# Two-pass attentions without pass-one sums: values and a ones column moving, outputs by query, in a two-block transformer on one Trainium2 core

## The chip, the cores and the metric

The kernel runs on one core of one Trainium2 chip, in one launch. The metric is device time in microseconds (us), median of the runs. The engines are TensorE (PE, matmuls; its weight loads are PEld), VectorE (DVE), ScalarE (ACT), GpSimd (POOL) and SyncE (SP, which issues most DMAs).

## What is computed

Two blocks over 512 tokens of width 1024, all in f32. The first block has an even layer (attention with 8 heads over 512 tokens and 256 context tokens, beside a convolution) and an odd layer (a recurrence in two directions, beside attention over a neighbourhood), each with adaptive modulation and followed by an expert-choice mixture of 16 experts. The second block has a forgetting attention (16 heads, causal, with a bias from cumulated gates), a feed-forward net, a sparse attention (16 heads, 2 groups of keys; a compressed, a selected and a window branch, each scaled by a gate) and another feed-forward net. Of the attentions this matters:

```
s = q @ k.T * scale            # plus bias, causal mask
p = softmax(s, -1)             # over the keys of one query
o = p @ v                      # by head
o_sparse = g0 * o_c + g1 * o_s + g2 * o_w
mod = silu(c) @ ada_w[i] + ada_b[i]     # six chunks of 1024: sh1, sc1, g1, sh2, sc2, g2
gate, idx = top_k(softmax(h @ router).T, cap)   # routing; g2 * (experts' output) is added to x
```

## The kernel before

One launch runs the stages one after another: the modulation's first chunks and the norm; the inputs of the even layer; the even attention; its output projection; routing and experts (the first mixture); the odd layer; routing and experts; the forgetting attention; a feed-forward net; the sparse attention; a feed-forward net. Matmuls that need f32 accuracy are split into high and low parts in a reduced type (f32r) and made as three products, or are made in f32, which stands in the trace as two matmul records, two passes.

**Two passes of attention.** Scores are needed with queries on the partitions for the maximum and the sum, and with keys on the partitions for the product with V. Pass one (`first`, in `even_first`, `fa_project` and `ns_first`) makes s = -q k by query block i; `Lse.take` (from L506) has DVE make the row's minimum and ACT the exponential of all scores, whose `accum_out` is the row's sum. `Lse.rows` turns -log(sum) - minimum into three bf16 parts, and a matmul with a selector (`add`, L542) adds them to the scores of pass two, so that the exponential of pass two is normalised already. Pass one takes the high and the low product of each score: KA and KL in the later attentions (L766 and L767, L1161 and L1162), three products of high and low parts in the even one (L1471 and, for context queries, L1474). Pass two (`second`) makes scores by key block j (L797 to L799, L1193 to L1195, L1500), the exponential PT on ACT, 128 keys by up to 512 queries, and the products: V's 64 columns are stationary, PT moves, and the two heads of a pair write the two halves of the partitions of one PSUM bank:

```
nc.tensor.matmul(ob[0][HALF[u], qs], lhsT=V[jj][:, h * 64:(h + 1) * 64], rhs=t[:, qs], ...)
```

These are L819, L1214, and L1518 and L1521 in the even layer. The bank then holds the output by feature, as the output projection wants it. In the sparse attention the two branches b and the compressed branch (PcT times vc) add up in one bank; the gates are in the row term (`lG`).

**What sets the order.** `attend` weaves pass one of the groups still to come with pass two of those that are through, step by step, with a manual schedule for PE and ACT. `along` and `interleave` weave two generators of steps with a ratio. A projection's PE work stands in the program order of such steps. PT has eight buffers, PSUM banks are named by use: bk, tb and ob.

**Even inputs.** `even_stage` interleaves `even_inputs` with `ada_steps` (L1643): seven modulation chunks, each of two halves of four loads (aw, 512 KB, on SP's queue) and 16 matmul passes a half (L1663). Chunks 2 and 5 go to HBM through a store on POOL's queue and are read back by rows where they are used (`mod_parts`, L1709).

**Routing** (in `moe`). Squares on ACT, the scaling of x for the gather on DVE (L1781), stored to HBM (L1785) on POOL's queue; transposes of x (L1796), logits (L1803, L1811), softmax, then eight rounds of a top-k search on DVE, index matmuls (L1854) and gathers (L1896) on POOL's queue. The experts' weights (mw, 1 MB) are on SP's queue.

**Odd attention** (`odd_attend`). It is woven with the recurrence. For each pair of heads p and query block i, head by head: scores (L2323 local, L2324 context) on the 64 partitions of the head, bias on DVE, maximum, exponential e with its sum on ACT, the sum's reciprocal on the diagonal of a tile dg (POOL, L2332); matmuls of e with dg transpose and normalise in one (L2342), ACT copies (L2344) and the products with V follow (L2355). `Later` puts off the second and third part by some steps.

## Time and profile before

| | us |
|---|---|
| median of 3 runs | 3947.52 (3941.67 to 3952.7) |
| the profiled execution | 3948.89 |
| its span in the trace | 3947.1 |
| PE busy | 3625.0 (92%) |
| DVE, ACT, POOL busy | 2090.8, 1588.8, 491.6 |
| mean granted PE clock | 0.953 |

The stages in the trace of that execution, in us from the start of the span: even inputs 47 to 273; the heads of the even attention and pass one of its first two groups 273 to 366; the rest of the even attention 366 to 504; its output projection to 570; routing to 617 and experts to 1249; odd layer to 1990, in it the odd attention woven with the recurrence from 1591 to 1780; routing to 2026 and experts to 2501; norm and projection of the forgetting attention to 2687, pass one of its first group from 2637 on; its attention to 2791; feed-forward to 3185; keys and queries of the sparse attention to 3298, pass one of its first group to 3361, its attention to 3546, output projection to 3580; feed-forward to the end.

A row of the timeline has the start, the length, the engine, the line, the operation with out<-in by the names of the program, the stationary operand (partitions*columns) and the moving one, a count of like instructions in a run, and in brackets the idle time before with what ended it. Matmuls are pipelined: the distance from start to start is what one costs, its length is more.

### The profile page before, as it was taken

The numbers are of one execution on the slowest core, as the hardware profiler recorded it, in microseconds if no ns is written. First come the engines' busy times: TensorE is split into PE (matmuls) and PEld (weight loads), VectorE is DVE, ScalarE is ACT, GpSimd is POOL, SyncE is SP. The second block draws the span as 40 slices with busy tenths as digits, with TensorE's granted clock in tenths as the row PEclk, the third lists the DMA queues.
The fourth block names the chain that finished last, engine by engine and source line by source line (L and its number), as shares of the span: only waits on it lengthen the run. The fifth ranks groups of instructions, "written<-read, shape, count | busy, mean of one in ns | idle before, by whom it ended". The sixth has DMA issues, their size and how long they took to land.

```text
span 3947.1 us, 53296 instructions
## 1 busy us (share of the span) xinstructions
PE 3625.0 (92%) x21365; PEld 2471.7 (63%) x21365; DVE 2090.8 (53%) x3363; ACT 1588.8 (40%) x2687; POOL 491.6 (12%) x603
## 2 busy tenths in 40 slices
PE   7998997999998989798779888899999998999999
PEld 4666574656564778575533323476788876667887
DVE  4747437777777554646342212564455556425444
ACT  3356534655554632341211000367433336644232
POOL 1442010000001231323010000310000012000000
PEclk8998998999998999898989999999999999999999
DMA  7440037888884361215579999422222230003232
GB/s 239 136 145 17 17 142 284 352 313 348 309 334 176 134 219 39 89 43 162 202 308 399 416 408 411 163 83 91 86 96 95 77 126 17 1 28 114 89 102 70
DMA packets 264344, 678.69 MB, mean 172 GB/s; under 512 B 16048, under 2 KB 142016, under 8 KB 214816
## 3 DMA queue, kind: packets, MB, share of 16 engines
q1 hardware_dynamic: 256832, 653.48, 45.3%
q0 software_dynamic: 7264, 21.80, 1.7%
q8 instruction: 168, 2.75, 0.3%
q14 instruction: 80, 0.66, 0.0%
HBM read 641.86 MB, written 32.83 MB: 171 GB/s over the span
## 4 chain that ended last, share of the span: by engine, by line
PE 47%; DMA 12%; DVE 4%; ACT 2%; issue 1%; POOL 1%; SPq 0%; POOLq 0%; DVEq 0%; ACTq 0%
PE bk L374 31%; DMA mw<-in_moe_w_dram 9%; DMA aw<-in_ada_w_dram 2%; PE bk L2011 2%; PE ob L1214 1%; PE bk L2342 1%; PE tb L1193 1%; PE bk L1663 1%; PE bk L2380 1%; PE tb L542 1%; DVE wl L351 1%; PE tb L1194 0%; PE ob L374 0%; DMA w<-in_a_w_in_dram 0%; PE rb L2547 0%
## 5 line engine op out<-in xcount | busy, mean ns | idle before, releaser
L351 DVE TENSOR_TENSOR wl<-w,wh 128x1024 fp32r<-128x1024 f32 (+2 forms) x157 | 256.4, 1637 | 276.0 <-ACT wh L350 275.5
L350 ACT CAST wh<-w 128x1024 fp32r<-128x1024 f32 (+2 forms) x157 | 215.5, 1375 | 377.5 <-PE bk L374 325.6
L351 DVE TENSOR_TENSOR wpl<-mw,wph 128x1024 fp32r<-128x1024 f32 x256 | 302.0, 1220 | 31.9 <-ACT wph L350 23.2
L374 PE MATMUL bk<-xTh,wh 128*128 128x512 f32 x704 | 274.3, 391 | 6.2 <-DVE xTl L354 6.2
L350 ACT CAST wph<-mw 128x1024 fp32r<-128x1024 f32 x256 | 258.2, 1047 | 49.2 <-PE bk L1938 31.0
L374 PE MATMUL bk<-xTh,wl 128*128 128x512 f32 x704 | 274.4, 390 | 0.0
L374 PE MATMUL bk<-xTl,wh 128*128 128x512 f32 x704 | 274.3, 390 | 0.0
L2011 PE MATMUL bk<-mw,xgT 128*64 128x512 f32 x1024 | 238.7, 602 | 26.7 <-DMA mw<-in_moe_w_dram 25.8
L2047 PE MATMUL bk<-mw,hidT 128*64 128x512 f32 x1024 | 248.5, 612 | 2.9 <-DMA mw<-in_moe_w_dram 2.2
L2011 PEld LDWEIGHTS bk<-mw,xgT 128*64 128x64 f32 x1024 | 70.0, 137 | 179.0 <-issue 126.3
L1938 PE MATMUL bk<-wph,xgPh 128*96 128x512 f32 x512 | 162.3, 397 | 1.3 <-ACT xgPh L1915 1.3
L1938 PE MATMUL bk<-wph,xgPl 128*96 128x512 f32 x512 | 160.6, 395 | 0.0
L1938 PE MATMUL bk<-wpl,xgPh 128*96 128x512 f32 x512 | 158.5, 394 | 0.0
L2047 PEld LDWEIGHTS bk<-mw,hidT 128*64 128x64 f32 x1024 | 72.2, 139 | 136.4 <-issue 124.1
L374 PEld LDWEIGHTS bk<-xTh,wh 128*128 128x128 f32 x704 | 132.7, 188 | 34.1 <-DVE xTl L354 6.6
L374 PEld LDWEIGHTS bk<-xTl,wh 128*128 128x128 f32 x704 | 132.6, 188 | 27.4
L374 PEld LDWEIGHTS bk<-xTh,wl 128*128 128x128 f32 x704 | 132.5, 188 | 27.5
L1896 POOL DMA_INDIRECT xg<-moe_xn,IDX x32 | 31.8, 994 | 878.1 <-PE tb L1908 849.2
L374 PE MATMUL bk<-wl,gTh 128*128 128x512 f32 x352 | 136.9, 389 | 0.0
L374 PE MATMUL bk<-wh,gTh 128*128 128x512 f32 x352 | 136.9, 389 | 0.0
L374 PE MATMUL bk<-wh,gTl 128*128 128x512 f32 x352 | 136.9, 389 | 0.0
L253 POOL TENSOR_TENSOR hr<-hr,mhalf 128x4 f32<-128x4 f32 (+3 forms) x77 | 91.6, 1196 | 260.8 <-DVE hr L485 255.5
(771 smaller groups left out, 8207.5 us busy)
## 6 DMA issues: line engine op xcount, KB each, us to landing
mw<-in_moe_w_dram SPq DMA_DIRECT2D x384, 1024.0 KB, 11.1
aw<-in_ada_w_dram SPq DMA_DIRECT2D x96, 512.0 KB, 4.6
w<-in_f_w_up_dram SPq DMA_DIRECT2D x40, 1024.0 KB, 5.1
w<-in_f_w_down_dram SPq DMA_DIRECT2D x16, 1024.0 KB, 4.9
w<-in_a_w_in_dram SPq DMA_DIRECT2D x24, 512.0 KB, 3.6
w<-in_od_w_in_dram SPq DMA_DIRECT2D x15, 512.0 KB, 4.6
w<-in_ev_w_in_dram SPq DMA_DIRECT2D x12, 512.0 KB, 4.9
rw_bk<-bk SPq DMA_DIRECT2D x8, 768.0 KB, 4.2
```

Source lines behind the costliest of these rows:

```text
L253: return self.nc.gpsimd.tensor_tensor(t, t, self.mhalf[:p].to_broadcast([p, n]), op=ALU.pow)
L350: nc.scalar.copy(h, src)
L351: nc.vector.tensor_sub(l, src, h.bitcast(F32))
L374: self.nc.tensor.matmul(out, lhsT=L[a], rhs=R[b], start=start and n == 0, stop=stop and n == len(pairs) - 1)
L542: self.k.nc.tensor.matmul(s, lhsT=self.k.selb[0:self.nr, h:h + 1].to_broadcast([self.nr, 128]), rhs=LT, start=False, stop=stop)
L1193: nc.tensor.matmul(s[:, q0:], lhsT=KA[:, b, kv, sl], rhs=QA[:, h, q0:], start=True, stop=False)
L1214: nc.tensor.matmul(o[HALF[u], 128 * jj:], lhsT=V[jj][:, b, kv * 64:(kv + 1) * 64], rhs=t[:, 128 * jj:], start=b == 0 and jj == 0, stop=False)
L1663: nc.tensor.matmul(ps[32 * g:32 * g + 32, :], lhsT=k.silc[:, kk, :], rhs=w[:, kk - k0, :], start=kk < 4, stop=kk >= 4)
L1938: at = nc.tensor.matmul(ps[hf], lhsT=t[a][:, kk, :], rhs=parts[b][:, kk % MOE_WK, hf * 512:hf * 512 + 512], start=kk + n == 0, stop=kk + n ...
L2011: nc.tensor.matmul(ps[64 * hf:64 * hf + 64, :], lhsT=t[:, kk, :], rhs=w[kk // 2][:, kk % 2, hf * 512:hf * 512 + 512], start=kk == 0, stop= ...
L2047: at = nc.tensor.matmul(px[64 * dh:64 * dh + 64, :], lhsT=hTx(q, c), rhs=w2[q][:, c, dh * 512:dh * 512 + 512], start=q + c == 0, stop=q + ...
L2342: nc.tensor.matmul(ps[rr, j * 128:(j + 1) * 128], lhsT=e[:, c0:c0 + n], rhs=dg, start=True, stop=True)
```

## The change

1. `Lse` becomes `Least`. Pass one keeps the high product alone and only takes minima; exponentials, sums and logarithm go. The row term is minus the minimum.
2. V gets a 65th column of ones. `Outs.products` has the 128x128 blocks of PT stationary and the 65 columns of V moving, one matmul for each query block and key block (`o`, 65 columns a query block). The sum stands in the last column. `over` makes the reciprocal on DVE (with the gate in the sparse attention), a DVE product writes a tile O by query, and `turn` transposes O on PE a few steps later and splits it. In the sparse attention each branch has its own pair of banks, the compressed branch comes as products by query in two further banks, and four multiply-adds a head and branch on DVE sum up. PT has 6 buffers (even layer 4), the later attentions have 2 banks bk and 4 ob, and the output projection uses ob.
3. `EV_FIRST`: twelve steps of the even inputs come before the first modulation step. Chunk 5 of layer 0 leaves them and is made in the first routing (`gates`).
4. Routing: transposes and logits stand first in the program, one pow for all squares, the scaling of x is on POOL (128x1024, six and four times).
5. Odd attention: the scores of both heads stand first and alternate between the two halves of the rows; POOL scales e (128x512) by the reciprocal; transposes take the place of the matmuls with the diagonal; values at middle positions are cut so that every block has four whole products.

The diff, cut to its core:

```
-class Lse:
+class Least:
...
-        return lambda: nc.scalar.activation(e, e, AF.Exp, scale=-1.0, bias=mn, accum_out=self.sm[:, h, i:i + 1])
...
-        nc.scalar.activation(t, self.sm[:, h0:h1, :], AF.Ln)
-        nc.vector.tensor_sub(t, t, self.mn[:, h0:h1, :])
...
+        nc.vector.tensor_scalar(t, self.mn[:, h0:h1, :], -1.0, None, op0=ALU.mult)
...
+class Outs:
...
+    def products(self, o, t, v, i0, n, first, last):
+
+        for i in range(n):
+            self.k.nc.tensor.matmul(o[:, 65 * (i0 + i):65 * (i0 + i) + 65], lhsT=t[:, 128 * i:128 * i + 128], rhs=v,
+                                    start=first and i == 0, stop=last and i == n - 1)
+
+    def over(self, o, gate=None):
+
+        nc = self.k.nc
+        v = o[:, 0:65 * self.nt].rearrange("p (i w) -> p i w", w=65)
+        r = self.P.tile([128, self.nt], F32, name="orr", tag="orr", bufs=4)
+        nc.vector.reciprocal(r, v[:, :, 64])
+        if gate is not None:
+            nc.vector.tensor_mul(r, r, gate)
+        return v[:, :, 0:64], r
...
+    def turn(self, bank):
+        nc = self.k.nc
+        for O, dst in self.due:
+            i = 0
+            for h, l, n in dst:
+                ps = bank()
+                for j in range(n):
+                    nc.tensor.transpose(ps[:, j * 128:(j + 1) * 128], O[:, i + j, :], self.k.ident)
+                split_copy(nc, h, l, ps[:, :n * 128])
+                i += n
+        self.due.clear()
...
-                            nc.tensor.matmul(s[:, :n], lhsT=QA[:, h, sl], rhs=KL[:, b, kv, :n], start=False, stop=False)
...
+                    def products(p=p, kv=kv, b=b, j=j, q0=q0, PT=PT, ob=ob):
+                        if j == 0:
+                            ob[:] = [k.obank(), k.obank()]
+                        for u in range(2):
+                            outs.products(ob[u], PT[u][:, q0:], V[j][:, b, kv, :], j, 4 - j, j == 0, j == 3)
                         if b == 0 and j == 0:
...
+                            outs.turn(k.bank)
...
+                                    nc.tensor.matmul(o[:, 64 * i:64 * i + 64], lhsT=PcT[c0:c0 + 32, p // 2, 128 * i:128 * i + 128],
+                                                     rhs=R["vc"][c0:c0 + 32, kv, :], start=True, stop=True)
...
+                    if j < 6:
+                        outs.products(o, t, E.V[j][:, h, :], 0, 4, j == 0, False)
+                    else:
+                        for u in range(2):
+                            outs.products(o, t[:, 256 * u:256 * u + 256], E.V[4 + u][:, h, :], 4, 2, False, u == 1)
...
-                interleave(even_inputs(k, E, hT, cqT, ckT, conv, ws), mods(M), EV_MODS)
+                steps = even_inputs(k, E, hT, cqT, ckT, conv, ws)
+                for _ in range(EV_FIRST):
+                    next(steps)
+                interleave(steps, mods(M), EV_MODS)
...
+            gates = ada_steps(k, Q, layer, (5,), 8, 1024, k.obank) if cs else iter(())
...
+                nc.gpsimd.tensor_scalar(t, x, ss[:, i:i + 1], None, op0=ALU.mult)
+                last = nc.gpsimd.dma_start(xnD[i * 128:(i + 1) * 128, :], t)
...
+            for c0, k0 in ((0, start[i]), (256, 512)):
+                for hd, r in enumerate(HALF):
+                    nc.tensor.matmul(ss[hd][:, c0:c0 + 256], lhsT=O.q[p][r, i * 128:(i + 1) * 128], rhs=O.k[p][r, k0:k0 + 256], start=True, stop=True)
...
+                nc.gpsimd.tensor_scalar(e, e, st[:, 2:3], None, op0=ALU.mult)
...
+                    for j in range(4):
+                        nc.tensor.transpose(ps[:, j * 128:(j + 1) * 128], e[:, j * 128:(j + 1) * 128], k.ident)
...
-        end_x = even_stage(k, lambda P: itertools.chain(ada_steps(k, P, 0, (2, 4, 3, 5), 5), ada_steps(k, P, 1, (1, 0, 2), 5)))
+        end_x = even_stage(k, lambda P: itertools.chain(ada_steps(k, P, 0, (2, 4, 3), 5), ada_steps(k, P, 1, (1, 0, 2), 5)))
```

How the change moves instructions is shown at three places. In these rows a name that ends in a number is a buffer, and a count at the end means so many alike in a run; the line numbers after the change are those of the changed file.

PE in the sparse attention, where the last products of a step stand between pass one (L1161 to L1163) and the next scores of pass two (L1193 to L1195, L542). Before:

```order
L1161 MATMUL bk<-KA,QA 128x128
L1162 MATMUL bk<-KL,QA 128x128
L1163 LDWEIGHTS identb
L1163 MATMUL bk<-causalb,identb 128x128
L1214 MATMUL ob<-PT,V_23540 64x512 x2
L1214 MATMUL ob<-PT,V_23541 64x384 x2
L1193 MATMUL tb<-QA,KA 128x128
L1194 MATMUL tb<-QA,KL 128x128
L1195 LDWEIGHTS causalb
L1195 MATMUL tb<-identb,causalb 128x128
```

PE at such a place with the change; L1200 and L1201 are pass one, L623 the products, L1229 to L1231 and L536 the scores of pass two:

```order
L1200 MATMUL bk<-KA,QA 128x512
L1201 LDWEIGHTS identb
L1201 MATMUL bk<-causalb,identb 128x128
L623 MATMUL ob<-V_23563,PT 128x65 x8
L1229 MATMUL tb<-QA,KA 128x256
L1230 MATMUL tb<-QA,KL 128x256
L1231 LDWEIGHTS causalb
L1231 MATMUL tb<-identb,causalb 128x128
L536 LDWEIGHTS selb
```

The low product of pass one is gone, and the products of two key blocks at a time with 64 stationary columns became, after each key block, one matmul of 65 moving columns for each query block.

PE in the odd attention. L2323 and L2324 are scores, L2342 the products with the diagonal, L2355 those with the values. Before:

```order
L2355 MATMUL bk<-PT,V_11150 64x128 x2
L2355 MATMUL bk<-PT,V_11151 64x128 x2
L2355 MATMUL bk<-PT,V_11152 64x128 x2
L2355 MATMUL bk<-PT,V_11153 64x128 x2
L2342 MATMUL bk<-dg,e 128x128 x8
L2323 MATMUL bk<-kT_11145,qT_11141 128x256
L2324 MATMUL bk<-kT_11145,qT_11141 128x256
L2323 MATMUL bk<-kT_11145,qT_11141 128x256
L2324 MATMUL bk<-kT_11145,qT_11141 128x256
```

PE in the odd attention with the change; L2375 are scores of the two heads in turn, L2393 transposes, L2404 products with the values, L2557 the recurrence:

```order
L2404 MATMUL bk<-PT,Vm_12642 64x128 x2
L2404 MATMUL bk<-PT,Vm_12645 64x128 x2
L2404 MATMUL bk<-PT,V_11155 64x128 x2
L2404 MATMUL bk<-PT,V_11156 64x128 x2
L2557 MATMUL rb<-q_13449,q_13480 32x32 x11
L2393 MATMUL bk<-c_all,e 128x128 x4
L2557 MATMUL rb<-q_13449,q_13480 32x32 x15
L2393 MATMUL bk<-c_all,e 128x128 x4
L2375 MATMUL bk<-kT_11148,qT_11144 128x256 x2
L2557 MATMUL rb<-q_13449,q_13480 32x32 x3
L2375 MATMUL bk<-kT_11148,qT_11144 128x256 x2
```

Eight products with the diagonal became four transposes a head, and the scores of both heads stand together.

POOL's queue in the first routing, up to the gathers (mod_5 is the chunk that the gates g and cg come from, moe_xn the scaled x). Before:

```order
L1785 DMA moe_xn<-xn 128x1024 x6
L1881 COPY Af<-Ax 128x8x64
L1883 COPY Af<-Ac 128x8x32
L1881 COPY Bf<-mod_3_918 128x8x64
L1883 COPY Bf<-mod_3_918 128x8x32
L1709 DMA g_4628<-mod_5 64x512 x2
L1709 DMA cg_4631<-mod_5 32x256 x4
L1896 DMA xg<-moe_xn,IDX 96x1024 x16
```

POOL's queue there with the change:

```order
L1852 TENSOR_SCALAR xn<-c_3856,ss 128x1024
L1853 DMA moe_xn<-xn 128x1024 x6
L1934 COPY Af<-Ax 128x8x64
L1936 COPY Af<-Ac 128x8x32
L1934 COPY Bf<-mod_3_1221 128x8x64
L1936 COPY Bf<-mod_3_1221 128x8x32
L1723 DMA mod_5<-ar 2x512
L1720 DMA ar<-in_ada_b_dram 2x512
L1723 DMA mod_5<-ar 2x512
L1759 DMA g_4631<-mod_5 64x512 x2
L1759 DMA cg_4634<-mod_5 32x256 x4
L1949 DMA xg<-moe_xn,IDX 96x1024 x16
```

The six scalings, the two stores of the chunk and the load of its bias now stand ahead of the gathers on this queue.

## Rows read from the trace of the kernel before

**Rows 1.** Busy us by stretch: length, PE, PEld, DVE, ACT, POOL, clock, DMA, GB/s
```profile
47.00:273.00 226.00, 210.45 (x1071) 136.39 (x1072) 129.98 (x177) 95.05 (x185) 90.37 (x98) 0.92 0.50 160
304.00:366.00 62.00, 52.16 (x292) 43.83 (x291) 51.18 (x108) 45.97 (x95) 22.63 (x33) 0.92 0.08 26
366.00:430.00 64.00, 58.97 (x227) 38.29 (x227) 48.65 (x65) 29.72 (x63) 0.00 (x0) 0.77 0.07 25
570.00:617.00 47.00, 25.44 (x164) 16.73 (x162) 31.87 (x96) 16.58 (x30) 21.33 (x32) 0.69 0.76 290
1591.00:1780.00 189.00, 156.18 (x2388) 129.18 (x2387) 112.02 (x234) 83.53 (x189) 53.14 (x62) 0.89 0.24 69
...
3298.00:3361.00 63.00, 51.14 (x278) 38.91 (x276) 47.99 (x119) 46.13 (x128) 16.26 (x28) 0.92 0.08 26
3361.00:3450.00 89.00, 86.44 (x584) 55.46 (x585) 39.92 (x100) 64.62 (x200) 7.33 (x12) 1.00 0.00 1
```

**Rows 2.** Timeline of PE, 570 to 592: start us, length us, instructions
```profile
571.25 1.96 PE L1770 MATMUL bk<-v,ones 128*128 128x16 f32 x16
...
581.41 0.60 PE L1796 MATMUL ob<-c_all,x 128*128 128x128 f32 x4
```

**Rows 3.** Timeline of PE, sparse attention, 3440 to 3451
```profile
3444.45 0.87 PE L1214 MATMUL ob<-PT,V 128*64 128x256 f32 x8
...
3447.35 0.40 PE L1162 MATMUL bk<-KL,QA 128*128 128x512 f32 x1
3447.59 0.23 PE L1163 MATMUL bk<-causalb,identb 128*128 128x128 bf16 x1
...
3449.19 1.73 PE L1214 MATMUL ob<-PT,V 128*64 128x512 f32 x8
```

**Rows 4.** Waits of PE, 47 to 273: total us, times, longest us
```profile
PE bk L1663 <- DMA aw<-in_ada_w_dram: 7.3, 4, 6.3
```

**Rows 5.** Timeline of PE, modulation chunk 5, 183 to 200
```profile
185.41 3.58 PE L1663 MATMUL bk<-aw,silc 128*32 128x512 f32 x16
...
193.82 0.59 PE L1671 MATMUL bk<-am,c_all 128*2 128x512 f32 x1 [3.23 <-ACT am L1666]
```

**Rows 6.** Even attention by line: duration ns min/median/max, first and last start
```profile
L1471 PE MATMUL wd<-KA,QA x192: 274/392/1415, 304.3 to 428.8; 96*128 96x512 f32 x96, 96*128 96x256 f32 x96
...
L1474 PE MATMUL wd<-KA,QA x48: 274/283/774, 317.6 to 431.8; 96*128 96x256 f32 x48
...
L1518 PE MATMUL bk<-PT,V x96: 592/592/1117, 384.2 to 499.9; 128*64 128x512 f32 x96
...
L1521 PE MATMUL bk<-PT,V x32: 379/379/431, 414.0 to 503.4; 128*64 128x256 f32 x32
```

**Rows 7.** Timeline of POOL, first routing, 570 to 618
```profile
597.43 0.50 POOL L1709 DMA_DIRECT2D cg<-mod  x1 [0.74 <-DMA moe_xn<-xn]
609.34 2.00 POOL L1896 DMA_INDIRECT xg<-moe_xn,IDX  x1 [11.40 <-DVE gtc L1876]
```

**Rows 8.** Waits of PE, first routing, 570 to 617
```profile
PE bk L1854 <- DVE ixf L1850: 11.9, 1, 11.9
```

**Rows 9.** Timeline of PE, odd attention, at 1640 and at 1770
```profile
1639.80 0.70 PE L2323 MATMUL bk<-kT,qT 64*128 64x256 f32 x2
1640.34 0.59 PE L2324 MATMUL bk<-kT,qT 64*128 64x256 f32 x2
...
1770.71 1.16 PE L2342 MATMUL bk<-dg,e 128*128 128x128 f32 x8
```

**Rows 10.** Waits of PE, odd attention, 1591 to 1780
```profile
PE bk L2342 <- POOL dg L2332: 8.6, 5, 3.8
PE bk L2342 <- ACT e L2329: 7.6, 3, 2.9
PE rb L2596 <- DVE x L2587: 6.8, 1, 6.8
```

**Rows 11.** Waits of PE, 3298 to 3361
```profile
PE ob L1161 <- ACT ob L512: 4.5, 4, 1.9
```

More of the change, by code (lines that the diff above doesn't have):

```diff
@@ L567, in simple @@
 def simple(steps):
-    for scores, exps in steps:
+    for scores in steps:
         scores()
-        exps()
         yield
@@ L594, in attend @@
                 now = (i, todo[i][0], todo[i][1])
-                now[2][0]()
+                now[2]()
                 i += 1
@@ L700, in fa_project @@
         nc.gpsimd.tensor_scalar(v[q], k.ident[q, None, 0:1].to_broadcast([64, 8, 512]), 0.0, None, op0=ALU.mult)
-    V = [P.tile([128, D], F32, name=f"V{i}") for i in range(4)]
+    V = [P.tile([128, 16, 65], F32, name=f"V{i}") for i in range(4)]
+    for v in V:
+        nc.gpsimd.memset(v[:, :, 64:65], 1.0)
     ncT = P.tile([128, 4, 16], F32, name="ncT")
@@ L766, in scores @@
                             nc.tensor.matmul(s[:, :n], lhsT=QA[:, h, sl], rhs=KA[:, h, :n], start=True, stop=False)
-                            nc.tensor.matmul(s[:, :n], lhsT=QA[:, h, sl], rhs=KL[:, h, :n], start=False, stop=False)
                             nc.tensor.matmul(s[:, sl], lhsT=k.identb, rhs=k.causalb, start=False, stop=True)
-                            late.append(S.take(s[:, :n], n, h, i, cb[h % 2][:, :n]))
-                    yield scores, lambda late=late: [f() for f in late]
+                            S.take(s[:, :n], n, h, i, cb[h % 2][:, :n])
+                    yield scores
         V_steps = k.dense_steps(xT, range(4), 8, split, [(k.wsrc(W, 2048), 1024, consume(2, 0))])
@@ L921, in shared_kv @@
     R["KL"] = S.tile([128, 2, 2, 512], F32R, name="KL")
-    R["V"] = [S.tile([128, 2, 128], F32, name=f"V{i}") for i in range(4)]
+    R["V"] = [S.tile([128, 2, 2, 65], F32, name=f"V{i}") for i in range(4)]
+    for v in R["V"]:
+        nc.gpsimd.memset(v[:, :, :, 64:65], 1.0)
     R["kcA"] = S.tile([128, 2, 224], F32R, name="kcA")
@@ L957, in consume @@
         pv = ps.rearrange("p (b s c) -> p b s c", b=2, s=2)
-        nc.scalar.copy(R["V"][i], pv[:, :, 1, :])
+        for b in range(2):
+            nc.scalar.copy(R["V"][i][:, b, :, 0:64], pv[:, b, 1, :].rearrange("p (g w) -> p g w", g=2))
         for b in range(2):
@@ L1275, in __init__ @@
         self.cv = P.tile([128, 4, self.CW - 30], F32, name="cv")
-        self.V = [P.tile([128, 512], F32, name=f"V{i}") for i in range(6)]
+        self.V = [P.tile([128, 8, 65], F32, name=f"V{i}") for i in range(6)]
+        for v in self.V:
+            nc.gpsimd.memset(v[:, :, 64:65], 1.0)
         self.KR = P.tile([128, 6, 32], F32, name="KR")
@@ L1804, in moe @@
                     hs = []
+            ss = Q.tile([128, nt], F32, name="ss")
+            xn = [Q.tile([128, D], F32, name="xn", tag="xn", bufs=nt) for _ in range(nt)]
+            for i, (x, t) in enumerate(zip(xs + cs, xn)):
+                nc.scalar.activation(t, x, AF.Square, accum_out=ss[:, i:i + 1])
+            nc.gpsimd.tensor_scalar(ss, ss, 1.0 / D, 1e-6, op0=ALU.mult, op1=ALU.add)
+            last = k.rsqrt(ss)
+            for i, (x, t) in enumerate(zip(xs + cs, xn)):
+                nc.gpsimd.tensor_scalar(t, x, ss[:, i:i + 1], None, op0=ALU.mult)
+                last = nc.gpsimd.dma_start(xnD[i * 128:(i + 1) * 128, :], t)
             lg = k.bank("lg")
@@ L1830, in moe @@
                 nc.scalar.copy(sel[32 * j:32 * j + 16, :], ps[0:16, 0:256])
+            for _ in range(4):
+                next(gates, None)
             val = Q.tile([np_, 64], F32, name="val")
@@ L1876, in moe @@
                 nc.vector.tensor_copy(gtc, ps[:, 0:16])
+            for _ in gates:
+                pass
         Af = P.tile([128, 8, NS], F32, name="Af")
@@ L2819, in fa_stage @@
     load_x(k, X, xD)
-    with k.work("faa", 3, 3, 4, 0, 2, 2, 1024), k.phase("faQ") as Q:
+    with k.work("faa", 3, 3, 2, 0, 2, 4, 1024), k.phase("faQ") as Q:
         fa_attend(k, ops, Q, k.T["a_w_out"], 1)
@@ L2863, in ns_stage @@
             turn = rows(NS_GROUPS[0])
-    with k.work("nsa", 3, 3, 4, 0, 2, 2, 1024), k.phase("nsQ") as Q:
+    with k.work("nsa", 3, 3, 2, 0, 2, 4, 1024), k.phase("nsQ") as Q:
         ns_attend(k, R, lse, first, rows, turn, Q, k.T["b_w_out"], 1, ns_compressed(k, Q, R, 1, k.bank))
```

225 lines of the change are left out of this document (98 added, 127 removed).

## The prediction

> **What bounds the kernel now.** I read the busy time by stretch first, one row per stage. TensorE (PE) is the limit nearly everywhere: 86.44 of 89.00 us in the middle of the last attention, 210.45 of 226.00 in the even inputs [rows 1]. So I ask of each stage whether PE is full; if it is, an instruction taken from PE is worth its own time, and one added costs it. Three stretches are different. In 304 to 366 VectorE (DVE) is busy 51.18 of 62.00 us beside PE's 52.16; in 1591 to 1780 PE has 33 idle us; in 570 to 617 (first routing) it is busy 25.44 of 47.00, and a chain of small steps sets the time [rows 1]. The second routing is the same work for four tiles of x instead of six. Then I read what PE waits for in the stages that the change touches [rows 4, 8, 10, 11], and last the timeline, to price one instruction by the distance between starts.
>
> The prices. An f32 matmul stands in the trace as two passes, and one pass with 128 stationary columns takes 0.112 us however little moves: sixteen passes with 16 moving columns take 1.96 us [rows 2], that is (1.96 - 0.27) / 15, where 0.27 is one pass to its end. By the 0.43 us of 512 moving columns below, 65 need 0.05 and lie inside that, so I take a 65-column product as 2 x 0.112 = **0.224 us**. An f32 transpose is one pass: four in 0.60 us, less the 0.27 of the last, 0.11 each [rows 2]. The form of before keeps the 64 value columns stationary, and two heads run side by side on two column halves: eight passes, four pairs, of 512 columns in 1.73 us, 0.43 a pair, and of 256 in 0.87, 0.22 a pair [rows 3]. The low product of pass one (KL) takes 0.24 us for 512 columns from its start to the next [rows 3]; for fewer columns I scale by columns down to 0.11 (384: 0.18, 256: 0.12, 128: 0.11), 0.65 for the four query blocks of a head.
>
> **The change, stage by stage** (us against the profiled execution's 3948.89).
>
> *Even inputs, -14.* Modulation chunk 5 goes to the routing: 32 passes, of which 16 take 3.58 [rows 5], so -7 on a full PE. A wait for ACT inside it (3.23 [rows 5]) may go too. Twelve input steps now stand before the first modulation step, so PE works while the first weights come: that wait is 6.3 of the 7.3 [rows 4]. I take -7, -6 and -1. Lower end -7 (the wait moves to the next load), upper -20.
>
> *Even heads, 304 to 366, -8.* Pass one drops two of three products: of 192 + 48 passes [rows 6] 128 + 32 go, 64 of 512 columns at 0.24 and 96 of 256 at 0.12, 27 us in all; half of that, 13, lies here. The exponentials of pass one leave ACT. But DVE's minima stay, and 51.18 of 62.00 us [rows 1] is a floor, so at most -11. Bounds -3 and -11.
>
> *Even attention, 366 to 504, +15.* Before: 96 passes of 512 columns in 48 pairs at 0.43 and 32 of 256 in 16 pairs at 0.22 [rows 3, 6]: 24 us. After: 224 products x 0.224 = 50. So +26, and 24 transposes +3, and the other half of pass one -13. Reciprocals and scaling on DVE lie beside PE (DVE 48.65 of 64.00 [rows 1], and that with the convolution, which ends there). 366 to 430 ran at a granted clock of 0.77 [rows 1]; how the new mix is clocked I can't see, so bounds +3 and +28.
>
> *First routing, +5.* The squares' scaling goes from DVE to POOL and logits come first: up to -6, since the top-k chain that PE waits 11.9 for [rows 8] starts sooner. Against it, chunk 5's eight 512 KB loads stand behind eight 1 MB loads on SP's queue, and its two stores and the six gate loads stand on POOL's queue ahead of the gathers. Before, POOL had the gate loads done at 597.43 and sat idle 11.40 us until the first gather at 609.34 [rows 7]. 12.6 MB at the 290 GB/s of this stretch [rows 1] are 43 us, so the weights land at 613 at the latest; part of the first 8 MB comes before 570, and I take 608. Then the last passes, a store, a load and the gather's issue, some 615. Bounds -6 (all inside the idle time) and +12.
>
> *Odd attention, 1591 to 1780, -25.* There are 32 blocks of one head. A block's scores are four f32 passes on 64 rows, 0.54 from the first product to the second, which is alike [rows 9]; now the two heads' products alternate row halves. The trace has no such pair of 256 columns; the nearest are column halves, which do run side by side [rows 3]. So between 0 and half: half, 32 x 0.5 = -17. The normalising matmuls (eight passes, 1.16 [rows 9]) become four transposes at 0.11: about -0.6 each, -19. The diagonal that PE waits for (8.6 [rows 10]) goes; in its place POOL scales 512 columns instead of 128, so that wait may stay. PE had 156.18 busy of 189.00 [rows 1], and its waits on the recurrence (6.8 for x, the largest [rows 10]) get less cover when attention work shrinks. Of 36 I keep two thirds. Bounds -5 and -40.
>
> *Second routing, -3*, the same scaling without a moved chunk. Bounds 0 and -6.
>
> *Forgetting attention, +11.* A head pair's products took 0.87 + 1.73 = 2.6, and take 20 x 0.224 = 4.5 now; they also come in four runs, not two, and a run's end costs some 0.15 (0.60 for four transposes at 0.11 [rows 2]), so 2.2 x 8 pairs = +17.6. Transposes 32 x 0.11 = +3.5; KL 16 heads x 0.65 = -10.4. The projection ahead of it is full of PE work too, so all of KL counts. No output projection is left to fill the last wait: +1 here. Bounds +5 and +16.
>
> *Sparse attention, +16.* Sixteen times 2.2 = +35; transposes +3.5; the compressed branch as eight more products a pair, half of them side by side on row groups, +4 (0 to 8); KL 32 x 0.65 = -21. Before the attention, 3298 to 3361, PE waited on ACT's pass-one exponentials (4.5 for the banks ob alone [rows 11]); these go, DVE is next with 47.99 of 63.00 [rows 1], so -6. Bounds +7 and +24.
>
> The sum is -14 - 8 + 15 + 5 - 25 - 3 + 11 + 16 = **-3**. The profiled execution lies 1.4 above the median of the runs, 3947.52, so I give **3945**.
>
> One rule speaks against the change. The Trainium skill, "TensorEngine Tiling (Array Packing)", section "When to Use Tiling", says that with a moving operand 64 wide or less one should swap, making it stationary, and use two column tiles; that is the form of before. By that rule alone each product doubles, +24 even, 8 x 2.6 = +21 and 16 x 2.6 = +42 instead of the +26, +18 and +35 above, and the sum would be +5, 3953. The rows' prices are what I take.
>
> **Rivals.** A difference of 0.3%, 12 us, is about what a measurement of this kernel can tell from none.
> 1. *Little moves* (3936 to 3959): the attentions' dearer products eat what inputs and odd stage give. For it: the prices of the products are rows of this trace, and gains and losses are of one size. 0.36.
> 2. *PE relief counts in full* (faster). The odd stage follows PE's work to -38, the even inputs reach -20: 13 + 6 more, 3926. For it: in 1591 to 1780 16 us of the waits are the attention's own (8.6 diagonal, 7.6 exponential [rows 10]). Against: these waits have heirs on POOL and ACT. 0.36.
> 3. *The recurrence becomes the bound in 1591 to 1780* (slower). Its chain of DVE and PE steps is woven with the attention; if it needs the 189 us by itself, the removed 36 us turn into waits, and only -5 is left: 3965. It decides once PE's waits for x, q and AMk grow by more than 12 us. For it: 6.8 already waited in one place [rows 10]; against: half of the 33 idle us are the attention's own waits. 0.2.
> 4. *The attentions cost their upper bounds*, because the many short products keep the low clock that 366 to 430 showed: +13, +5 and +8, 3971. 0.08.
>
> That gives faster 0.36, same 0.36, slower 0.28. The bounds all together would reach 3880 to 4012; but they are independent, and adding their half widths by squares (7, 4, 12, 9, 17, 3, 6, 9) gives 27. I leave out a tenth at each end, take 33 for it as some terms can be wrong in kind, and get 3911 to 3977. The likeliest case's own range is 3936 to 3959.
>
> **What would show it.** The distance between two 65-column passes: 0.112 if right, and near 0.06 if weight loads hide, which would take some 70 us (704 products, two passes each) from the sum and make me wrong by far. The stretch of the odd attention about 25 us shorter, waits on POOL's scaling at most 9 us. The sparse attention from its first query pass to the last product 16 us longer. In the first routing a gather at 615 behind the gate loads; if it comes before 609, that term is wrong. PE in the even pass one well under DVE's busy time.

## The result

The changed kernel takes 3994.43 us (median of 4 runs, 3972.86 to 4004.68) against 3949.91 (median of 4 runs of the kernel before): ratio 1.0109, interval 1.0074 to 1.0144, or +43 us. That is 1.1% slower, clear of the noise; I had forecast 3945, 3 us less than before, with a range from 3911 to 3977. The profiled execution of the change took 3999.19 us, 50 more than that of before. From the starts of the first matmuls of each stage in the two traces:

| stage | before | after | difference | predicted |
|---|---|---|---|---|
| even inputs | 224.8 | 215.4 | -9 | -14 |
| even heads and first pass one | 94.2 | 90.1 | -4 | -8 |
| even attention, pass two | 137.5 | 167.4 | +30 | +15 |
| first routing, to the experts' first matmul | 46.0 | 61.5 | +15 | +5 |
| odd stage from the queries on | 554.0 | 551.5 | -2 | -25 |
| second routing | 35.1 | 36.2 | +1 | -3 |
| forgetting attention, pass one to output projection | 179.7 | 179.1 | -1 | +11 |
| sparse attention, pass one to output projection | 275.1 | 293.9 | +19 | +16 |

The rest, some +2, is scattered over stages that the change doesn't touch.

The busy time by stretch of the changed kernel (columns as in [rows 1], counts in brackets): heads and first pass one; pass two in three pieces; first routing; odd attention; sparse attention. In [rows 1] the stretches from 304, 366, 570, 1591 and 3361 answer to them.

```profile
293.00:351.00 58.00, 42.52 (x205) 34.55 (x203) 49.84 (x108) 20.66 (x38) 21.70 (x33) 0.87 0.09 28
...
346.00:421.00 75.00, 69.43 (x240) 53.94 (x241) 49.05 (x67) 11.44 (x18) 0.00 (x0) 0.50 0.02 6
421.00:434.00 13.00, 11.30 (x68) 8.26 (x67) 7.73 (x17) 4.35 (x9) 0.00 (x0) 1.00 0.35 121
434.00:519.00 85.00, 80.77 (x518) 65.23 (x517) 13.94 (x32) 35.00 (x57) 0.00 (x0) 0.96 0.00 1
...
585.00:648.00 63.00, 34.61 (x202) 17.07 (x202) 29.12 (x86) 13.61 (x24) 36.36 (x38) 0.77 0.82 307
1625.00:1802.00 177.00, 145.77 (x2234) 115.85 (x2233) 113.76 (x236) 83.03 (x187) 82.93 (x61) 0.85 0.20 60
3388.00:3480.00 92.00, 88.59 (x712) 73.45 (x721) 47.31 (x165) 30.38 (x72) 7.33 (x12) 0.98 0.01 1
```

Read the clock column of the second row: for 75 us from the start of pass two in the even attention PE had half its clock (0.50, the level of 1.2 GHz), though it was busy 69.43 of them. Before, the stretch from 356 to 387 was at half clock and the next at full:

```profile
356.00:387.00 31.00, 26.30 (x81) 17.90 (x81) 18.51 (x28) 13.35 (x28) 0.00 (x0) 0.50 0.00 1
387.00:421.00 34.00, 29.75 (x150) 18.84 (x148) 31.46 (x44) 20.19 (x42) 0.00 (x0) 1.00 0.00 1
```

The waits of PE in the changed kernel's first routing and odd attention (total us, times, longest us) answer to [rows 8] and [rows 10]:

```profile
PE tb L1961 <- DMA xg<-moe_xn,IDX: 15.5, 1, 15.5
PE bk L1905 <- DVE ixf L1901: 5.5, 1, 5.5
...
PE bk L2393 <- POOL e L2383: 24.4, 14, 4.4
PE rb L2645 <- DVE x L2636: 3.6, 2, 1.8
```

The first routing now waits 15.5 us for the gathered rows, the odd attention 24.4 us for POOL's scaling of e.

### The profile page after: what moved, and what is told of

Read it like the earlier page. It is cut to its first block, busy times and chain, and to the rows that moved or that the text cites. A ratio compares the mean times of both kernels' runs of the same rounds, so it can differ in the third digit from the quotient of the medians.

```text
span 3997.1 us, 54148 instructions
## 1 busy us (share of the span) xinstructions
PE 3660.0 (92%) x21909; PEld 2572.6 (64%) x21933; DVE 2122.8 (53%) x3578; ACT 1432.3 (36%) x2199; POOL 548.8 (14%) x623
## 5 line engine op out<-in xcount | busy, mean ns | idle before, releaser
L2064 PEld LDWEIGHTS bk<-mw,xgT 128*64 128x64 f32 x1024 | 70.1, 138 | 180.7 <-issue 130.5
## 6 DMA issues: line engine op xcount, KB each, us to landing
mw<-in_moe_w_dram SPq DMA_DIRECT2D x384, 1024.0 KB, 10.6
```

Source lines behind the costliest of these rows:

```text
L2064: nc.tensor.matmul(ps[64 * hf:64 * hf + 64, :], lhsT=t[:, kk, :], rhs=w[kk // 2][:, kk % 2, hf * 512:hf * 512 + 512], start=kk == 0, stop= ...
```

## The experiments

Every kernel below is the kernel before with one part of the change, or a part altered, so the differences are against before on the same chip. Below, "low clock" is the time that the profile grants PE 0.50, and 0.1% is 3.9 us.

### The even attention: 2 by 2, and a filler

`even_alone` takes both halves of the change (pass one with minima alone, L1471 to L1474; products of 65 moving columns), `even_one` pass one alone, `even_two` the products alone:

```
 even_one:  Least, scores of the high product alone; products as before
            (the division by the sum is left out)
 even_two:  Lse and three products in pass one as before
-nc.tensor.matmul(ob[0][r, :], lhsT=E.V[jj][:, v], rhs=t, start=jj == 0, stop=jj == 5)
+outs.products(o, t, E.V[j][:, h, :], 0, 4, j == 0, False)
```

> The kernel before with the changed even attention alone (minima in pass one, products of 65 moving columns). In the changed kernel the heads gave -4 us and the attend stage +30. Expected +26 us, within 12, with about 75 us of low clock from the start of pass two on. If the long low clock was an accident of that run, the stage has some 45 us of low clock or less and the total is +12 to +16.

> The kernel before with the even layer's new pass one (minima from the high product) but the products of before, 64 stationary columns in two column halves; the division by the sum is left out. Theory (the short products hold the clock low): the clock recovers some 30 us into the stage as before, -20 to -30 us. Rival (the thinner pass one ahead of it sets the low clock): 70 us or more of low clock here too, -5 to -15 us.

> The kernel before with the even layer's products of 65 moving columns but its old pass one (three products, exponentials and sums stay, the division by the sum comes on top). Theory (the short products hold the clock low once it has fallen): 60 us or more of low clock from the start of pass two, stage of the attend 45 to 55 us longer than before, total +40 to +50. Rival (only the thin new pass one together with them does it): about 30 us of low clock, +26 to +35.

| | ratio (interval) | us | pass two | low clock in it |
|---|---|---|---|---|
| before and fourteen kernels with this stage unchanged | | | 131 to 138 | 20 to 38 |
| even_one | 0.9979 (0.9969 to 0.9989) | -8 | 127 | 30 |
| even_alone | 1.0077 (1.0050 to 1.0104) | +30 | 168 | 76 |
| even_two | 1.0153 (1.0127 to 1.0179) | +60 | 182 | 85 |

The next three fences are the busy time by stretch of pass two, from where the clock fell; read the clock column. First even_alone:

```profile
358.00:432.00 74.00, 69.07 (x240) 53.69 (x241) 48.78 (x67) 10.72 (x17) 0.00 (x0) 0.50 0.01 3
432.00:446.00 14.00, 12.30 (x74) 9.18 (x73) 8.01 (x17) 5.03 (x10) 0.00 (x0) 0.98 0.31 114
```

The same view of even_one:

```profile
352.00:375.00 23.00, 19.25 (x57) 11.28 (x57) 16.56 (x22) 4.95 (x7) 0.00 (x0) 0.50 0.08 24
375.00:486.00 111.00, 102.12 (x429) 53.26 (x427) 48.76 (x79) 44.01 (x74) 0.00 (x0) 0.94 0.04 15
```

And of even_two:

```profile
358.00:450.00 92.00, 86.89 (x306) 70.66 (x307) 50.97 (x73) 32.55 (x67) 0.00 (x0) 0.50 0.01 2
450.00:551.00 101.00, 94.03 (x601) 74.86 (x600) 21.14 (x48) 45.81 (x78) 0.00 (x0) 0.98 0.04 16
```

All three fall to the low clock at the same point, the end of the heads, where PE waits for the last norm on DVE (qn, 2.8 us in even_alone and even_one, 1.1 us in even_two) and a few us later for the row terms. With the old products the clock is back after 23 us; with the 65-column products it stays low for 74 and 92, with the thin pass one and with the old one. So it is the products, not the pass one ahead of them, and the long low stretch is no accident of one run: the changed kernel and even_alone both had 75 us of it, and even_alone's +30 is what I expected. "The products" here means that whole half of the change: with the 65 columns come their order (one key block at a time), the transposes, the division on DVE and 4 PT buffers for 8, and I took none of these apart. I had the sign of even_one right but expected -20 to -30: pass one gave some -6 of its 13 us in pass two and as much ahead of it, and the total (-8, interval -4 to -12) agrees with that. even_two went as its theory had it in clock (85 us low for 60 or more) and stage (50 us over the usual 132); its total, +60, lies above the +40 to +50 expected.

Does the new mix draw the clock down, or does it only fail to bring it back? `even_fill` puts 32 useless matmuls of 512 columns ahead of even_alone's first scores of pass two:

```
+if g == 0 and j == 0 and h == 0:
+    w = k.tbank()
+    for _ in range(32):
+        nc.tensor.matmul(w, lhsT=KA[0:96, 0, 0, 0:128], rhs=QA[0:96, 0, 0, 0:512], start=True, stop=True)
```

> The changed even attention alone, with 32 matmuls of 512 moving columns of no use put before the first scores of pass two (14 us at the low clock). Theory (after dense work the clock is back, and the short products then keep it): the low stretch of 75 us becomes 30 us or less, and the total is 5 to 15 us below that of the same kernel without them, +15 to +25 against before. Rival (the mix itself draws the clock down): low stretch of 60 us or more after the useless matmuls, total +40.

Busy time by stretch of pass two in even_fill:

```profile
363.00:374.00 11.00, 10.86 (x34) 8.69 (x35) 1.36 (x3) 0.00 (x0) 0.00 (x0) 0.70 0.01 1
374.00:417.00 43.00, 35.94 (x225) 27.85 (x223) 41.28 (x57) 9.56 (x16) 0.00 (x0) 1.00 0.00 1
417.00:448.00 31.00, 28.24 (x89) 20.85 (x90) 8.47 (x18) 7.73 (x13) 0.00 (x0) 0.51 0.14 51
```

The clock comes back within the filler and the same mix then runs 43 us at full clock. It falls again at 417, in a wait of PE for the convolution (4.36 us, `L1412 <- DVE cv`), and stays low for 31 us. Pass two without the filler took 152 us instead of 168. The total did not follow: 1.0081 (1.0053 to 1.0110), as even_alone; the filler itself cost 11 us, and its ten runs spread from 3948 to 3999, so I can't say in how many of them the clock did as in this profile. In all four profiles with the new products (the changed kernel, even_alone, even_two, even_fill) the low clock ended 1 to 4 us after a run of f32 matmuls with 512 columns began, those of the convolution's norm; in the changed kernel:

```profile
417.14 5.57 PE L1363 MATMUL tb<-cv,on 128*128 128x512 f32 x8
422.15 0.92 PE L1517 MATMUL wd<-KA,QA 96*128 96x512 f32 x2
```

### The first routing: POOL's queue

`first` has the twelve input steps alone (EV_FIRST), `gates` also moves chunk 5, `route` is the new order of routing with the scaling on POOL alone, `gates_act` is `gates` with the chunk's and the gates' DMAs on ACT's queue:

```
-nc.gpsimd.dma_start(mod[c][:, hf * 512:(hf + 1) * 512], row)
+(nc.scalar if (i, c) == (0, 5) else nc.gpsimd).dma_start(mod[c][:, hf * 512:(hf + 1) * 512], row)
...
-g2 = mod_parts(k, E, mod, 5, 0, 2, "g2")
+g2 = mod_parts(k, E, mod, 5, 0, 2, "g2", nc.scalar if cs else nc.gpsimd)
```

> The kernel before with twelve steps of the even inputs ahead of the first modulation step, chunk 5 still among them. Theory: PE's wait of 6.3 us for the first weights goes and nothing takes its place: -4 to -8 us. Rival: the wait moves to a later load or to the convolution's end: 0, within 3.

> The kernel before with that and with chunk 5 moved into the first routing, the routing's scaling of x still on DVE. Theory (stores and gate loads ahead of the gathers on POOL's queue): even inputs -10, the gather some 15 us later than before, first routing +12 to +16, total +2 to +6 us. Rival (in the changed kernel it was POOL's scaling of x that held the gather): routing within 4 us of before, total -8 us.

> The kernel before with the changed routing alone: scaling of x on POOL, 2.85 us a tile, transposes first, chunk 5 where it was. Theory: six scalings take 17 us, so the stores of x land about 20 us later, after the indices are known, and the gather waits for them: first routing +5 to +12, second routing 0 to +2. Rival (the stores stay inside the top-k's time): -2 to -6 us.

> Chunk 5 in the first routing, twelve input steps first, but the chunk's stores, its bias loads and the gate loads go to ACT's queue instead of POOL's. Theory (these held the gathers up): first routing within 5 us of before instead of +17, total -8 to -12 against before. Rival (PE's second half of the chunk holds the gather's transposes): routing +8 to +12, total within 3 of before.

| | ratio (interval) | even inputs | first routing |
|---|---|---|---|
| before | | 224.8 | 46.0 |
| first | 1.0004 (0.9995 to 1.0014) | 218.8 | 45.1 |
| gates | 1.0022 (1.0006 to 1.0039) | 212.4 | 61.9 |
| route | 1.0004 (0.9986 to 1.0022) | 224.7 | 45.2 |
| gates_act | 0.9990 (0.9970 to 1.0010) | 213.2 | 53.6 |

In `first` the inputs give their 6 us, and the median of its ten runs doesn't show it (+2, interval -2 to +6). Its profile can't say why: it is of the fastest of the ten, 20 us shorter than the profile of before, of which 9 lie in the second experts, which nothing touched. So -4 to -8 for the total is not shown. Moving the chunk gives 6 us in the inputs and costs 17 in the routing, and `gates` is 9 us slower than before (interval +2 to +15). `route` rejects the theory for it that POOL's slow scaling holds the gather; the scaling costs nothing and gains nothing that can be measured. POOL's timeline in the changed kernel shows what does:

```profile
609.18 3.29 POOL L1853 DMA_DIRECT2D moe_xn<-xn  x6
...
625.01 0.55 POOL L1723 DMA_DIRECT2D mod<-ar  x1 [10.69 <-DVE gtc L1927]
628.11 0.51 POOL L1720 DMA_DIRECT2D ar<-in_ada_b_dram  x1 [2.55 <-DMA mod<-ar]
630.95 0.51 POOL L1723 DMA_DIRECT2D mod<-ar  x1 [2.33 <-DVE ar L1722]
631.45 0.85 POOL L1759 DMA_DIRECT2D g<-mod  x1
632.80 0.54 POOL L1759 DMA_DIRECT2D g<-mod  x1 [0.50 <-DMA mod<-ar]
633.33 1.97 POOL L1759 DMA_DIRECT2D cg<-mod  x4
635.61 1.41 POOL L1949 DMA_INDIRECT xg<-moe_xn,IDX  x1 [0.30 <-issue]
```

A store, a bias load that waits until it has landed, a second store, six gate loads, then the gather: 10.6 us of queue, which began some 3 us after the indices were there. The second store waits for a sum on DVE that needs both the bias load (landed at 629.86) and PE's last passes of the chunk (ended at 629.89), so two chains end there together. The gather itself then took 9.7 us from issue to landing, against 5.1 before: some 5 of the 15 us that the routing lost. With these DMAs on ACT's queue (`gates_act`) it lands in 4.4, and it leaves POOL as soon as the indices are there, as the row of POOL's timeline shows. But ACT, which now stands behind the gate loads, casts the experts' weights late, and after them the gathered rows that PE needs:

```profile
590.92 1.01 POOL L2001 DMA_INDIRECT xg<-moe_xn,IDX  x1 [25.86 <-DVE IDX L1971]
```

The row of ACT's timeline, in the same kernel:

```profile
600.15 3.88 ACT L350 CAST wph<-mw 128x1024 fp32r<-128x1024 f32 x4 [6.88 <-DMA g<-mod]
```

So half of the 17 us went, and half became a wait of PE for ACT (7.8 us, `L2043 <- ACT xgPh`). The routing (+8) and the total (-4, interval -12 to +4) came out nearer to the rival than to the theory, but not by the rival's mechanism: PE's passes of the chunk were done (594.3) before the gathered rows were there (595.3).

### The odd attention

`odd_alone` has the changed odd attention alone, `odd_dve` scales e on DVE. `odd_dve_aw` splits the loads of the modulation that is woven behind the attention (ODD_AW) into 256 KB in two buffers, `odd_dve_aw2` has two buffers of 512 KB; the space comes from single buffers in `odd_out`. `aw2` is that alone.

```
-nc.gpsimd.tensor_scalar(e, e, st[:, 2:3], None, op0=ALU.mult)
+nc.vector.tensor_scalar(e, e, st[:, 2:3], None, op0=ALU.mult)
...
-ODD_AW = 1, 1024
+ODD_AW = 2, 1024      # odd_dve_aw: 2, 512
...
-g = mod_row(k, Q, mod, 2, 0, "g", c0, 256, 2)   # and ox 3, ot 2 buffers
+g = mod_row(k, Q, mod, 2, 0, "g", c0, 256, 1)   # and ox 2, ot 1
```

> The kernel before with the changed odd attention alone. Theory: POOL's scaling of e (1.57 us for 128x512 in the changed kernel, 24.4 us of PE waits on it) eats what PE saves: -5 us against before, within 8; PE waits on POOL e about 24 us again. Rival (the recurrence is the bound): also near 0, but the waits stand at the recurrence's x, q and S.

> The same odd attention, e scaled on DVE instead of POOL. Theory: DVE does 128x512 in about 0.4 to 0.5 us, the wait of 24 us goes, -20 to -30 us against before. Rival (recurrence is the bound): within 5 us of the run with POOL, and the waits move to the recurrence's results.

> The changed odd attention with e scaled on DVE, and the modulation weights that are woven behind it loaded in pieces of 256 KB into two buffers instead of 512 KB into one. Theory (what the attention saves is given back as waits for these loads, 25 us): waits on aw fall to 12 us or less, and the total is 8 to 15 us below the run with DVE alone, -18 to -26 against before. Rival (the recurrence's chain is the bound there): waits move to the recurrence, total within 4 us of the run with DVE alone.

> The changed odd attention with e on DVE, the modulation weights in two buffers of 512 KB, so that the two matmuls of a load still run side by side (the pieces of 256 KB made them run one by one, 29 us more of PE). Theory (the attention's gain is given back as waits for these loads): waits on aw under 8 us without more PE time, odd stage 15 to 25 us shorter than with DVE alone. Rival (the recurrence's chain sets the end): odd stage within 6 us of the run with DVE alone.

> The kernel before with these two buffers alone. Theory: waits on aw fall from 22 to under 8 us, -10 to -20 us. Rival: within 4 us of before, the waits move to the recurrence's results. With the run beside it this tells what the odd attention gives when nothing behind it waits for loads.

Times from the first scores to the first matmul of the output projection (attention), and from there to the routing (rest), in the profiles:

| | ratio (interval) | attention | low clock | rest |
|---|---|---|---|---|
| old attention, ten kernels and before | | 192 to 200 | 38 to 79 | 205 to 213 |
| the changed kernel (POOL) | | 182 | 56 | 211 |
| odd_alone | 0.9995 (0.9981 to 1.0009) | 204 | 73 | 203 |
| odd_dve | 0.9973 (0.9956 to 0.9990) | 184 | 61 | 213 |
| odd_dve_aw | 0.9986 (0.9967 to 1.0005) | 187 | 65 | 217 |
| odd_dve_aw2 | 0.9935 (0.9917 to 0.9953) | 190 | 75 | 191 |
| aw2 | 0.9938 (0.9926 to 0.9951) | 194 | 44 | 193 |

POOL needs 1.57 us for a scaling that DVE does in 0.48 (median of 32 each). The row of the changed kernel's e on POOL (min/median/max ns):

```profile
L2383 POOL TENSOR_SCALAR e<-e,st x32: 1559/1566/2527, 1633.8 to 1795.7; 128x512 f32<-128x512 f32 x32
```

In odd_alone PE waited 18.8 us for POOL's e, as the theory said, but also 20.6 for the recurrence in that stretch (15.1 before, 6.6 in the changed kernel), so its -2 alone doesn't decide between theory and rival. With DVE the total is 11 us below before (4 to 17), half of what I had expected, and 9 below the form with POOL, where the intervals just overlap. A single profile tells little about the attention's stretch: the same form with POOL took 182 us in the changed kernel and 204 in odd_alone. With DVE the stretch goes with the low clock, 184 us at 61 of low clock, 187 at 65, 190 at 75, and 196 at 89 and 92 in best1 and best2 below. That the gain is given back to the modulation's loads is rejected. Waits of PE for these loads, before and in aw2:

```profile
PE bk L1663 <- DMA aw<-in_ada_w_dram: 22.2, 15, 4.1
```

```profile
PE bk L1760 <- DMA aw<-in_ada_w_dram: 10.0, 6, 3.9
```

Two buffers gave the old attention 24 us (aw2), twice what these waits lost, and the rest I haven't traced. They gave the new one less: from odd_dve to odd_dve_aw2 the waits fell from 25 to 9 us and the total by 15, and odd_dve_aw2 and aw2 end within 2 us of each other. odd_dve_aw was a badly made experiment: its 256 KB pieces hold one block of the contraction each, so two column tiles no longer ran side by side, and L1663's work rose from 30 to 59 us of PE while its waits fell from 25 to 3.

For the last question two kernels differ in the odd attention alone, beside `first`, `gates_act` and the two buffers: `best2` with the new one on DVE, `best3` with the old one.

> Two buffers for the modulation weights, twelve input steps first, chunk 5 in the first routing with its stores and gate loads on ACT's queue, and the changed odd attention with e on DVE. Attentions of before. If the odd attention's relief is given back by the granted clock (61 to 89 us of low clock in its stretch against 38 to 79 with the old one): within 6 us of the run beside it, -24 to -32 against before. Rival (it gives its PE work back in full): 15 us below the run beside it.

> The same with the odd attention of before: the two buffers gave -24, the inputs with the chunk moved and ACT's queue -4: -24 to -32 against before.

best2: 0.9933 (0.9913 to 0.9953), best3: 0.9958 (0.9942 to 0.9974). In the profiles both need the same 196 us for the attention. The busy time by stretch of best2:

```profile
1582.00:1778.00 196.00, 159.14 (x2284) 126.47 (x2286) 127.67 (x271) 85.78 (x191) 32.91 (x31) 0.76 0.25 71
```

The same stretch of best3:

```profile
1582.00:1778.00 196.00, 162.62 (x2451) 134.18 (x2451) 114.42 (x239) 85.00 (x191) 51.96 (x61) 0.88 0.25 73
```

With 167 fewer passes PE is busy 3.5 us less, at a clock of 0.76 instead of 0.88, and idle as long as before (37 and 33 us). In these two profiles the work that was taken away came back as slower work. By the medians best2 is 9 us faster than best3, with intervals that overlap, so in how many executions the clock did as here is not shown. best2 gave the -24 to -32 that I expected, best3 (-17, interval -10 to -23) did not.

One more part of the expected gain never existed. The scores of the two heads do run side by side on the row halves, when no other matmul stands between them. In the changed kernel eight passes in a row took 1.60 us (partly at the low clock), but four of one head, with the recurrence's matmuls behind them, 1.13:

```profile
1666.20 1.60 PE L2375 MATMUL bk<-kT,qT 64*128 64x256 f32 x8
...
1719.21 1.13 PE L2375 MATMUL bk<-kT,qT 64*128 64x256 f32 x4
1720.27 0.31 PE L2557 MATMUL rb<-q,q 32*32 32x32 f32 x6
1720.51 1.13 PE L2375 MATMUL bk<-kT,qT 64*128 64x256 f32 x4
```

Counting passes that start within 0.03 us of another, 40 of 128 were the second of a pair, and before it was 32 already: there, too, the scores of the two heads often stood next to each other. That is 8 passes of 0.21 us, 2 us instead of 17.

### The later attentions, and a sum of parts

> The kernel before with the changed sparse attention alone. In the changed kernel its pass one gave -3 and attention with output projection +22. Expected +19 us, within 6; PE passes of the products 0.112 us apart.

> The kernel before with the changed forgetting attention alone. By the prediction's terms +11 us; by the stage times of the changed kernel -0.6 (pass one in the projection -6.5, attention and output projection +5.9). If the latter, within 3 us of before.

> Twelve input steps first, the changed odd attention with e on DVE, two buffers for the modulation weights, and the changed forgetting attention; even and sparse attention and routing as before. If the parts add up: -6 for the inputs, -25 to -35 for the odd stage, 0 for the forgetting attention, -30 to -40 against before. Rival (the odd stage is bound by its recurrence): -8 to -15.

`ns`: 1.0032 (1.0017 to 1.0048), +13 us; its profile has the stage at +19 as in the changed kernel. `fa`: 1.0009 (0.9996 to 1.0022), no difference that can be measured. One term of the sparse attention went the other way. Before, PE waited in pass one for ACT's exponentials, 4.5 us for the banks ob [rows 11] and 4.1 for the banks bk:

```profile
PE bk L1161 <- ACT bk L512: 4.1, 2, 2.3
```

They went, and other waits stood in their place in the changed kernel's stretch of pass one, 3327 to 3389:

```profile
PE tb L1179 <- POOL e L1171: 7.2, 3, 6.9
PE bk L1200 <- DVE lmn L507: 3.0, 4, 1.7
PE ob L1200 <- DVE lmn L507: 2.0, 2, 1.8
```

L1171 is POOL's part of the compressed branch, L507 DVE's minima. The prices, in the sparse attention of the changed kernel:

```profile
3397.71 1.50 PE L623 MATMUL ob<-V,PT 128*128 128x65 f32 x12
...
3400.25 1.06 PE L623 MATMUL ob<-V,PT 128*128 128x65 f32 x8
3401.24 1.11 PE L1255 MATMUL bk<-vcD,PcT 32*128 32x64 f32 x16
```

Twelve passes less eight, (1.50 - 1.06) / 4, are 0.11 a pass, as forecast. `best1` (first, fa, odd_dve, two buffers): 0.9954 (0.9941 to 0.9966), -18, less than aw2 alone and short of the -30 to -40 of the sum; its odd attention had 89 us of low clock, in a profile of its slowest run (3939.95). best3, with the old odd attention, is by its median also short of aw2. So the gains don't add up, and whether the clock is the reason is not shown. The losses do, roughly: even_alone, gates, route, odd_alone, fa and ns come to 30 + 9 + 2 - 2 + 4 + 13 = +56, the whole change to +43 (interval 29 to 57).

aw2, odd_dve_aw2 and best2 beat both kernels, by 24 to 26 us against before and some 68 against the change. aw2 is the one to take: one number and three buffers.

## Why the prediction was wrong, step by step

By the stage table three terms failed: odd attention (-25, measured -2), even attention (+15, measured +30) and first routing (+5, measured +15). They make 48 of the 53 us between the forecast of -3 and the profile's +50; the other terms were off by 5 us or less, but for the forgetting attention (12 us the other way), and nearly cancel. The step that failed in the even attention is the price of its work at full clock; in the odd attention it is the pairing of the scores, POOL's scaling let off as a wait, and the clock; in the routing the length of the chain ahead of the gather.

- **The price of a 65-column product was right**, 0.107 to 0.112 us a pass in every attention at full clock. By the sum of starts the sparse attention's products went from 39.5 to 70.1 us (+31, predicted +35), the forgetting one's from 20.1 to 34.3 (+14, predicted +18). Most of the error of 4 is the 0.15 that I added for the ends of runs: the next matmul starts inside them. The Trainium skill ("TensorEngine Tiling (Array Packing)", "When to Use Tiling") says to swap a moving operand of 64 columns, so that it is the stationary one, and to use two column tiles. The runs agree: with 65 columns moving the products cost 1.7 and 1.8 times as much here.
- **Even attention, +15**: +30. The count was right, the step that failed was to price all of it at full clock, with the clock put into the bounds (+3 to +28). Alone the stage cost 35 us more than its usual 132, outside these bounds. even_one and even_two show that the products lengthened the low stretch from about 23 to 75 us and more. My fourth rival named this mechanism; I gave it 0.08.
- **First routing, +5**: +15. I named the stores and gate loads ahead of the gathers, but took one store and one load for the chain. It is store, bias load, store, six loads, with waits of 2.3 to 2.6 us between the first three: 10.6 us of queue. That the gather itself would land 5 us later I had not reckoned with at all. gates (61.9) and route (45.2) show that moving the chunk alone makes the difference.
- **Odd attention, -25, the largest miss**: -2, with the attention's own stretch 10 us shorter and the rest of the stage longer. Three steps failed. Scores were paired in part already: 40 paired passes for 32, -2 for -17, and the sentence that the trace has no such pair was wrong. POOL's scaling was let off with "that wait may stay": at 1.57 us it took 24.4 us of waits where diagonal and exponential had had 16.2 [rows 10]. And the granted clock, which I left out, took back much of the rest in the profiles of best2 and best3; by their medians it is less. The transposes did what was forecast: the diagonal's products took 46 us in best3, the transposes 27 in best2. My third rival, the recurrence as the bound, isn't what happened in the changed kernel: PE's waits for it fell from 15 to 7 us there, and rose only from 12 to 17 between best3 and best2. In odd_alone they were 21, so for that run it stays open.
- **Even inputs, -14**: -6 for the first wait, as forecast, and -6 for the chunk; -9 in the changed kernel's own profile. **Even heads, -8**: -4, DVE's floor, as the bound of -3 said.
- **Forgetting attention, +11**: -1. Products +14, transposes +3, KL -11, and the waits of PE fell from 7 to 5 where I had added 1. That makes +3, which `fa` alone (+4, interval -2 to +9) allows; where the stage in the profile gets the other 4 us I haven't traced.
- **Sparse attention, +16**: +19 in the profiles, +13 alone by the median. The term holds, but in part by luck: products +31 for +35, the compressed branch 0 for +4 (8.1 and 8.3 us by the sum of starts), and PE's waits in pass one rose from 12 to 15 us where I had taken 6 off, as POOL's and DVE's work stood behind ACT's. The errors cancel.
- The range came from adding errors as if they were independent. The granted clock touched two of the three large ones in the same direction, the even attention (shown by the runs) and the odd one (seen in two profiles).

## What to carry to other kernels

A stage that PE fills with short products right after a wait should be priced at both clock levels, and the profile asked what stood there when the clock last came back. In the even attention it came back 1 to 4 us after runs of f32 matmuls with 512 columns began, and stayed low through 74 to 92 us of scores and 65-column products; the sparse attention ran the same kind of products at 0.98. PE work that is removed beside waits may come back as a lower clock, so measure the stretch, not PE's busy time, and in more than one profile. When DMAs move onto a queue, write out the chain of waits ahead of the next instruction that matters, and look for single-buffered loads first: two buffers for one weight tile were worth more than the whole change meant to win.

## What the runs showed that I had not expected

- The granted clock stayed at half for 74 to 92 us while PE was busy 93% and more of that time with scores and 65-column products, and the same mix ran at full clock for 43 us once it had it (even_fill).
- POOL's scaling by a column costs 1.57 us for 128x512 and 2.85 us for 128x1024 f32 (L1852 of the changed kernel), DVE's 0.48 for 128x512.
- Single 512 KB loads that each wait for the one buffer to come free cost 22 us of PE waits over 24 loads; with a second buffer the waits were 10 us and the time 24 us less (0.9938).
- The gathered rows took 9.7 us from issue to landing when six gate loads had been issued just ahead of them on POOL's queue, and 4.4 us when these loads were on ACT's.
